# Rotary tables, squares and weight roundings reordered in a kernel's first stretch

## The chip, the cores and the metric

The kernel runs on one core of a Trainium2 chip. The metric is the time of one execution in device microseconds. A core has a matrix engine (TensorE, PE in the profile), a vector engine (VectorE, DVE), an engine for activation functions (ScalarE, ACT), a general engine (GpSimd, POOL) and SyncE (SP), which here issues most of the loads. Each engine works through its own queue in order; ScalarE and GpSimd have DMA queues of their own beside SyncE's.

## The reference

Two layers of a decoder on 512 tokens of width 1024, in float32. What matters here is the beginning of the first one: a norm, one projection whose columns are queries (512), keys (128), values (128) and a gated convolution (3 x 512), and attention in which queries and keys are normed per head and rotated.

```python
def _rope_tables(positions):
    inv_freq = ROPE_THETA ** (-jnp.arange(0, HEAD_DIM, 2, dtype=jnp.float32) / HEAD_DIM)
    ang = positions.astype(jnp.float32)[..., None] * inv_freq
    return jnp.cos(ang)[:, :, None, :], jnp.sin(ang)[:, :, None, :]

h = _rms_norm(x, mix_norm[i])                       # x * rsqrt(mean(x^2) + eps) * gain
q, k, v, cb, cc, cx = _split(h @ w_in, HY_SPLITS)
q = _apply_rope(_rms_norm(q.reshape(b, s, 8, 64), q_norm), cos, sin)
k = _apply_rope(_rms_norm(k.reshape(b, s, 2, 64), k_norm), cos, sin)
# sliding-window attention with sinks, a gated short convolution, an output projection,
# a gated MLP, a per-layer embedding; then a second layer with gated linear attention
```

## The kernel before

Every float32 matrix product is made of three products of rounded operands: each operand is split into a rounded part (hi, an ACTIVATE on ScalarE) and its rest (lo, a subtraction on VectorE), and TensorE adds hi x hi, hi x lo and lo x hi. For weights the split is `cut` (lines 151 and 153), or, in the first stretch, `rounded_w` (line 555), which rounds and returns a function that makes the rest (line 557). The tiles are `raw` (two buffers of 1 MB), `wh` and `wl` (three each).

`mixer0` begins the first layer. Its order is written out by hand inside `tc.manual_schedule` for TensorE, VectorE and ScalarE: the x blocks are transposed (`turn`, line 535, two PSUM banks `turns`), scaled and rounded (`rounded_x`, line 542), their rests made (`rest_x`, line 546), x kept in float32 (`kept`, line 560), while `keys_values` (line 519) and `queries` (line 528) run over the 8 blocks k of the width. Queries 0 to 3 run here; queries 4 to 7 need another 1 MB of weights and run behind, through `mm3` (lines 177 to 179). Ahead of all this `idle` issues matmuls whose result goes nowhere (line 237): four in `setup`, three behind the first transposition. `square` (line 563) sums x squared for the row norm on ScalarE; `end_norm` makes the row factors rtok of them (lines 208 and 209).

What stands outside the hand-written order is placed by a planner that goes by the order of the program text and by its own estimate of when each instruction is ready; it may put such instructions between those of the hand-written order. `tc.issue_after(ins)` keeps instructions behind `ins` on its engine. Before the change the rounding of query weights 4 to 7, two of the four squares, the row norm and the rotary tables stood outside.

`rope_tables` loads the positions through GpSimd's queue (line 416), converts and transposes them (418, 420, 422), makes the angles (426), reduces each to a sine's range (437 to 445), takes sine and cosine on ScalarE (446), and multiplies them by the query and key norms' gains (459 to 464). The keys, scaled by rtok (line 676), are then normed and rotated (651 to 685), transposed by TensorE (667), and the attention and the convolution's projections (line 177 to 179 again, by `conv_in`) follow. The loads that GpSimd issues are held back until the last of x has landed (`late`, line 241).

## Time and profile before

| | |
|---|---|
| median of three runs | 1199.97 us (1198.24 to 1200.52) |
| the profiled execution | 1197.56 us, its span 1195.8 us |
| TensorE busy | 1186.5 us, 99% of the span |
| VectorE, ScalarE, GpSimd busy | 995.1, 693.6, 46.2 us |
| granted TensorE clock | 1.00 |

All times in a timeline are microseconds from the start of the span. The stretch that the change touches ends at about 46 us. A row of a timeline gives start, length, engine, line, operation, what it writes and reads, and in brackets how long the engine stood idle before it and what ended that. A matmul's row shows its length in the pipeline; how fast matmuls follow each other is read from their starts.

### The profile page before, as it was taken

To read this page: it belongs to the slowest core of one execution; us is meant where nothing else is said; L and a number is where in the kernel's file an instruction comes from. 1 tells how busy PE (TensorE), PEld (TensorE's weight loads), DVE (VectorE), ACT (ScalarE), POOL (GpSimd) and SP (SyncE) were. 2 spreads that over 40 slices of the span, in tenths; PEclk is the share of its full clock that TensorE was granted. 3 is DMA by queue.
4 is the path that set the end of the run, shared out by engine and by line. 5 is a ranking of instruction groups with operands and counts; after the bars stand their busy time and mean duration, and the time that the engine had idled before them with its cause. 6 is when DMAs were issued, how large, how long until landed. Compare 5 with 4: busy or idle time off the path is not lost.

```text
span 1195.8 us, 20221 instructions
## 1 busy us (share of the span) xinstructions
PE 1186.5 (99%) x8210; PEld 1077.5 (90%) x8210; DVE 995.1 (83%) x1597; ACT 693.6 (58%) x1140; POOL 46.2 (4%) x65
## 2 busy tenths in 40 slices
PE   9999999999999999999999999999999999999998
PEld 8777789999999989889988988899999999888887
DVE  4986687898999997889879876687989999988595
ACT  6666555556555744666664655555555656655374
POOL 2610000000000000000100000000000000000000
PEclk9999999999999999999999999999999999999999
DMA  7223222332323343422412212223233333323601
GB/s 223 76 80 93 75 89 71 102 111 101 112 83 113 107 141 98 129 74 65 146 59 70 84 59 71 88 74 117 93 112 101 106 107 114 125 89 98 211 1 71
DMA packets 113666, 117.77 MB, mean 98 GB/s; under 512 B 2936, under 2 KB 108594, under 8 KB 113572
## 3 DMA queue, kind: packets, MB, share of 16 engines
q1 hardware_dynamic: 112592, 115.75, 29.9%
q8 instruction: 64, 1.05, 0.4%
q0 software_dynamic: 592, 0.43, 0.3%
q10 hardware_dynamic: 388, 0.30, 0.1%
q14 instruction: 30, 0.25, 0.1%
HBM read 114.37 MB, written 2.10 MB: 97 GB/s over the span
## 4 chain that ended last, share of the span: by engine, by line
PE 86%; DVE 8%; ACT 3%; DMA 1%; issue 1%; POOL 0%; ACTq 0%; DVEq 0%
PE ps L177 7%; PE ps L178 7%; PE ps L179 7%; PE pa L179 6%; PE pa L178 6%; PE pa L177 6%; PE ps L1021 5%; PE ps L1023 5%; PE ps L1022 5%; PE ps L193 5%; PE ps L191 5%; PE ps L200 4%; PE pa L1023 2%; PE pa L1021 2%; PE pa L1022 2%; DVE wl L969 2%
## 5 line engine op out<-in xcount | busy, mean ns | idle before, releaser
L153 DVE TENSOR_TENSOR wl<-raw,wh 128x1024 fp32r<-128x1024 f32 (+2 forms) x132 | 153.8, 1168 | 35.9 <-ACT wh L151 33.7
L151 ACT ACTIVATE wh<-raw 128x1024 fp32r<-128x1024 f32 (+3 forms) x136 | 136.7, 1007 | 64.1 <-PE ps L178 26.9
L966 ACT ACTIVATE wh<-raw 128x1024 fp32r<-128x1024 f32 x90 | 95.8, 1065 | 128.1 <-DVE raw L993 80.2
L1084 DVE SCALAR_TENSOR_TENSOR zt<-z,vfa,zt 128x510 f32<-128x510 f32 (+1 forms) x176 | 131.0, 745 | 0.3
L969 DVE TENSOR_TENSOR wl<-raw,wh 128x1024 fp32r<-128x1024 f32 x90 | 110.1, 1223 | 17.0 <-ACT wh L966 16.0
L179 PE MATMUL pa<-b,wl 128*128 128x256 f32 x352 | 97.3, 276 | 0.1
L179 PE MATMUL pa<-a,wl 128*128 128x256 f32 x352 | 97.3, 276 | 0.0
L177 PE MATMUL pa<-a,wh 128*128 128x256 f32 x352 | 97.2, 276 | 0.0
L178 PE MATMUL pa<-a,wh 128*128 128x256 f32 x352 | 97.2, 276 | 0.0
L177 PE MATMUL pa<-b,wh 128*128 128x256 f32 x352 | 97.2, 276 | 0.0
L178 PE MATMUL pa<-b,wh 128*128 128x256 f32 x352 | 97.2, 276 | 0.0
L1082 ACT ACTIVATE zt<-z,vfb 128x512 f32<-128x512 f32 x88 | 71.5, 813 | 19.1 <-DVE z L1074 9.5
L191 PE MATMUL ps<-b,wh 128*128 128x512 f32 (+1 forms) x192 | 72.9, 383 | 0.0
L193 PE MATMUL ps<-b,wh 128*128 128x512 f32 (+1 forms) x192 | 72.2, 379 | 0.0
L179 PEld LDWEIGHTS pa<-b,wl 128*128 128x128 f32 x352 | 66.1, 188 | 0.3 <-DVE wl L153 0.3
L178 PEld LDWEIGHTS pa<-a,wh 128*128 128x128 f32 x352 | 66.1, 188 | 0.0
L178 PEld LDWEIGHTS pa<-b,wh 128*128 128x128 f32 x352 | 66.1, 188 | 0.0
L177 PEld LDWEIGHTS pa<-a,wh 128*128 128x128 f32 x352 | 66.1, 188 | 0.0
L177 PEld LDWEIGHTS pa<-b,wh 128*128 128x128 f32 x352 | 66.1, 188 | 0.0
L179 PEld LDWEIGHTS pa<-a,wl 128*128 128x128 f32 x352 | 66.1, 188 | 0.0
L1021 PE MATMUL ps<-four,wh 128*128 128x256 f32 x232 | 64.7, 279 | 0.0
L1023 PE MATMUL ps<-four,wl 128*128 128x256 f32 x232 | 64.1, 276 | 0.0
(537 smaller groups left out, 3698.9 us busy)
## 6 DMA issues: line engine op xcount, KB each, us to landing
raw<-in_ffn_w_up_dram SPq DMA_DIRECT2D x42, 1024.0 KB, 5.0
raw<-in_ffn_w_down_dram SPq DMA_DIRECT2D x13, 1024.0 KB, 5.1
raw<-in_gla_w_in_dram SPq DMA_DIRECT2D x8, 1024.0 KB, 5.4
raw<-in_hy_w_in_dram SPq DMA_DIRECT2D x7, 1024.0 KB, 5.0
raw<-in_ffn_w_down_dram SPq DMA_DIRECT2D x8, 768.0 KB, 4.9
raw<-in_ple_w_gate_dram SPq DMA_DIRECT2D x6, 1024.0 KB, 5.4
raw<-in_hy_w_out_dram SPq DMA_DIRECT2D x16, 256.0 KB, 3.9
raw<-in_gla_w_out_dram SPq DMA_DIRECT2D x4, 1024.0 KB, 5.2
```

Source lines behind the costliest of these rows:

```text
L151: nc.scalar.activation(hv, v, AF.Copy)
L153: self.rest_cut = nc.vector.tensor_tensor(lv, v, hv.bitcast(F32), ALU.subtract)
L177: mm(out, lh, rh, start=start, stop=False, **kw)
L178: mm(out, lh, rl, start=False, stop=False, **kw)
L179: mm(out, ll, rh, start=False, stop=stop, **kw)
L191: mm(out, lh, rh, start=first, stop=False, **kw)
L193: end = mm(out, lt, rt, start=False, stop=False, **kw)
L966: nc.scalar.activation(h, src, AF.Copy)
L969: nc.vector.tensor_tensor(l, src, h.bitcast(F32), ALU.subtract)
L1021: mm(out, wh, xh, start=first and j == 0, stop=False, **kw)
L1023: mm(out, wl, xh, start=False, stop=j == ND // 2 - 1, **kw)
L1084: nc.vector.scalar_tensor_tensor(out=y[:, tap:], in0=z[:, : S - tap], scalar=w[:, f : f + 1], in1=y[:, tap:], op0=ALU.mult, op1=ALU.add,)
```

## The change

- `rope_tables` becomes a generator in three parts. The first (positions, their transposition into the bank `turns[1]`, angles, the sine's argument) stands in the hand-written order ahead of `keys_values(4)`, behind the rest of key weights 6 and 7. It gives back the sine as a function, which is called behind the fourth square. The second part (the cosine's argument) follows, with its sine at once. The products with the gains stay behind the row norm.
- `square(2)` is issued ahead of the first part, `square(3)` behind the copies of x blocks 6 and 7, both in the hand-written order. The rest of key weights 6 and 7 moves ahead of the operands' transpositions.
- Query weights 4 to 7 are loaded as before. Their rounding is bound behind `square(3)` for 4 and 5, and behind the last copy of the values for 6 and 7.
- The scaling of the sinks by -1 is bound behind the normed keys.
- The first block of key and value weights is loaded by SyncE, third in its queue behind x block 0, and no longer by ScalarE's queue; the first norm's gains (`vec0`) go through ScalarE's queue and no longer through GpSimd's.
- Two idle matmuls stand behind the first transposition in place of three.

```diff
-        self.kvr = self.raw(ND, 256)
...
-            nc.scalar.dma_start(self.kvr[:, 0, :], a["hy_w_in"][0][:P, 512:768])
...
-        finish = self.columns("vec0", [f(a["mix_norm"])], self.nc.gpsimd)
+        finish = self.columns("vec0", [f(a["mix_norm"])], self.nc.scalar)
...
-    def rope_tables(self, pool):
+    def rope_tables(self, pool, bank):
...
-        ps = self.pa()
-        nc.tensor.transpose(ps[:, :NT], pf, self.ident[:NT, :NT])
+        nc.tensor.transpose(bank[:, :NT], pf, self.ident[:NT, :NT])
         pos = self.cf[:, P : P + NT]
-        nc.vector.tensor_copy(pos, ps[:, :NT])
+        nc.vector.tensor_copy(pos, bank[:, :NT])
+        (the loads of the gains g, moved here from behind the sines)
...
-            nc.scalar.activation(r, r, AF.Sin)
             sc.append(o)
+            yield lambda r=r: nc.scalar.activation(r, r, AF.Sin)
...
-        return C, Sn
+        yield C, Sn
...
-            kvr, wqr = self.kvr, self.raw(4, 512)
+            kvr, wqr = self.raw(ND, 256), self.raw(4, 512)
...
             load_x(0, 1)
+            load_kv(0, 1)
             load_q(0, 1)
...
-                self.idle(3)
+                self.idle(2)
...
                 square(0)
                 square(1)
+                square(2)
+                rest()
+                tables = self.rope_tables(mp, turns[1])
+                sine = next(tables)
                 keys_values(4, 0, 1, 2)
                 turn(6, 7)
                 rounded_x(6)
                 rounded_x(7)
-                rest()
                 rest_x(6)
                 rest_x(7)
                 last = [kept(6, on_act), kept(7, on_dve)]
+                squared = square(3)
+                sine()
+                next(tables)()
                 keys_values(5, 0, 1, 2)
...
-            wq47 = self.weights(w_in[:, 4:8, :512], 4, 512, by="a")
-            wq.update({k: wq47(k - 4, 0, 512) for k in range(4, ND)})
-            with tc.issue_after(last[0].ins):
-                square(2)
-                square(3)
+            wqr = self.raw(4, 512)
+            load(wqr, w_in[:, 4:8, :512])
+            with tc.issue_after(squared.ins):
+                rounded_w(wq, wqr[:, :2], 4, self.weight_tiles())()
             self.end_norm(sums=sums)
-            with tc.issue_after(last[1].ins):
-                C, Sn = self.rope_tables(mp)
+            C, Sn = next(tables)
...
-            nc.vector.tensor_scalar_mul(sink, sink, -1.0)
...
-                nc.scalar.activation(v, pkv[t][:, 128:], AF.Copy, scale=rt)
+                kept_v = nc.scalar.activation(v, pkv[t][:, 128:], AF.Copy, scale=rt)
                 vs.append(v)
+            with tc.issue_after(kept_v.ins):
+                rest = rounded_w(wq, wqr[:, 2:], 6, self.weight_tiles())
+            rest()
...
+            with tc.issue_after(normal.ins):
+                nc.vector.tensor_scalar_mul(sink, sink, -1.0)
```

More of the change, by code (lines that the diff above doesn't have):

```diff
@@ L418, in rope_tables @@
         nc.vector.tensor_copy(pf, pr)
-        ps = self.pa()
-        nc.tensor.transpose(ps[:, :NT], pf, self.ident[:NT, :NT])
+        nc.tensor.transpose(bank[:, :NT], pf, self.ident[:NT, :NT])
         pos = self.cf[:, P : P + NT]
-        nc.vector.tensor_copy(pos, ps[:, :NT])
+        nc.vector.tensor_copy(pos, bank[:, :NT])
+        g = pool.tile([P, 2, HD], F32, name="gqk")
+        for w in range(2):
+            self.late(g[:, w, :1])
+        nc.gpsimd.dma_start(g[:, 0, :], a["hy_q_norm"][0:1, :].partition_broadcast(P))
+        nc.gpsimd.dma_start(g[:, 1, :], a["hy_k_norm"][0:1, :].partition_broadcast(P))
         h = HD // 2
@@ L445, in rope_tables @@
             nc.vector.tensor_scalar(r, r, PI_SAFE, -PI_SAFE, op0=ALU.min, op1=ALU.max)
-            nc.scalar.activation(r, r, AF.Sin)
             sc.append(o)
+            yield lambda r=r: nc.scalar.activation(r, r, AF.Sin)
         sin, cos = sc
-        g = pool.tile([P, 2, HD], F32, name="gqk")
-        for w in range(2):
-            self.late(g[:, w, :1])
-        nc.gpsimd.dma_start(g[:, 0, :], a["hy_q_norm"][0:1, :].partition_broadcast(P))
-        nc.gpsimd.dma_start(g[:, 1, :], a["hy_k_norm"][0:1, :].partition_broadcast(P))
         C = pool.tile([P, NT, 2, HD], F32, name="ropeC")
@@ L562, in square @@
             def square(t):
-                nc.scalar.activation(junk, xin[t // 2][:, t % 2, :], AF.Square, accum_out=sums[:, t : t + 1])
+                return nc.scalar.activation(
+                    junk, xin[t // 2][:, t % 2, :], AF.Square, accum_out=sums[:, t : t + 1]
+                )
             on_act, on_dve = nc.scalar.copy, nc.vector.tensor_copy
@@ L684, in mixer0 @@
             kn = mp.tile([P, 8, HD], F32, tag="qn", name="kn", bufs=2)
-            nc.vector.tensor_tensor(kn, m1, rk.unsqueeze(2).to_broadcast([P, 8, HD]), ALU.mult)
+            normal = nc.vector.tensor_tensor(kn, m1, rk.unsqueeze(2).to_broadcast([P, 8, HD]), ALU.mult)
+            with tc.issue_after(normal.ins):
+                nc.vector.tensor_scalar_mul(sink, sink, -1.0)
             for k in range(4, ND):
```

## The prediction

> **What bounds the kernel now.** I read the page first, then the waits of TensorE, then the timeline of each engine over the first 60 us, where all of the change lies, and last the DMA issues of that stretch. The page and the waits of TensorE (what it waited for: us in total, times, longest):

> ```profile
> span 1195.8 us, 20221 instructions
> PE 1186.5 (99%) x8210; PEld 1077.5 (90%) x8210; DVE 995.1 (83%) x1597; ACT 693.6 (58%) x1140; POOL 46.2 (4%) x65
> PE pa L667 <- DVE kn L685: 2.1, 1, 2.1
> ```

> TensorE is busy for 99% of the span, so time falls only where TensorE stands still or where it works slowly, and rises only where it is made to wait. The list of its waits has the longest first, and that is one stall: the transposition of the normed keys, kn (line 667), waits for VectorE. TensorE's timeline shows its size (start, length, instruction, idle time ahead):

> ```profile
> 43.34 0.39 PE L178 MATMUL ps<-wl,a 128*128 128x512 f32 x1
> 43.57 0.39 PE L179 MATMUL ps<-wh,a 128*128 128x512 f32 x1
> 46.10 0.66 PE L667 MATMUL pa<-cf,kn 128*128 128x128 f32 x4 [2.14 <-DVE kn L685]
> ```

> These matmuls start 0.23 us apart (43.57 - 43.34). Without a wait the transposition would have started at 43.80, so 46.10 - 43.80 = 2.30 us are lost. Why kn is late is read from VectorE:

> ```profile
> 26.12 0.17 DVE L642 TENSOR_SCALAR sink<-sink 128x8 f32<-128x8 f32 x1 [3.55 <-DMA sink<-in_hy_sinks_dram]
> 28.12 1.22 DVE L153 TENSOR_TENSOR wl<-raw,wh 128x1024 fp32r<-128x1024 f32 x1
> 32.89 0.16 DVE L422 COPY cf<-pa 128x4 f32<-128x4 f32 x1 [0.15 <-PE pa L420]
> 33.09 0.68 DVE L426 TENSOR_SCALAR ang<-cf 128x32 f32<-128x32 f32 x4
> 37.15 0.29 DVE L442 SCALAR_TENSOR_TENSOR tabsin<-kksin,tabsin 128x128 f32<-128x128 f32 x1
> 37.48 0.23 DVE L445 TENSOR_SCALAR tabsin<-tabsin 128x128 f32<-128x128 f32 x1
> 43.08 1.11 DVE L655 TENSOR_TENSOR m<-kx,ropeC 128x512 f32<-128x512 f32 x1
> 44.29 1.02 DVE L660 TENSOR_TENSOR m<-m,m 128x512 f32<-128x512 f32 x1
> 45.35 0.69 DVE L685 TENSOR_TENSOR kn<-m,rq 128x512 f32<-128x512 f32 x1
> ```

> VectorE stands still for 3.55 us up to 26.12, at a scaling of the sinks whose load is late. Then it makes the rotary tables between 32.89 and 43.08, mixed with weight rests (the wl of line 153) and with the keys' sums, and only then the keys can be multiplied by ropeC. The tables end late, and kn with them.

> **The tables, part by part.** The position's transposition now stands in TensorE's order between the last of queries(2) and keys_values(4), and VectorE gets the steps up to the sine's argument right behind the rest of key weights 6 and 7, ahead of the operands' rests 6 and 7.

> ```profile
> 17.92 0.52 POOL L416 DMA_DIRECT2D pos_i<-in_positions_dram  x1
> pos_i<-in_positions_dram POOLq DMA_DIRECT2D x1, 2.0 KB, 2.5
> sink<-in_hy_sinks_dram POOLq DMA_DIRECT2D x1, 4.0 KB, 6.5
> 21.88 0.69 DVE L557 TENSOR_TENSOR wl<-raw,wh 128x512 fp32r<-128x512 f32 x1
> 19.52 0.56 POOL L641 DMA_DIRECT2D sink<-in_hy_sinks_dram  x1
> 23.17 0.99 PE L519 MATMUL pa<-wh,a 128*128 128x256 f32 x7
> ```

> The positions land at 17.92 + 2.5 = 20.4. The rest of weights 6 and 7 ends at 22.57, the conversion of so small a tile (no longer than the copy of 0.16) at about 22.8, and TensorE comes to this place at 23.17. So the new wait has 0.4 us to spare on VectorE's side and 2.4 us on the load's. The copy back (0.16), the angles (0.68) and the reduction follow. That reduction takes seven VectorE instructions like the two at 37.15 and 37.48, of 0.23 to 0.29 us and 0.33 apart: 2.0 us, an estimate. The sine's argument is then ready at about 23.4 + 0.2 + 0.7 + 2.0 = 26.3. All of this fills the 3.55 us in which VectorE stood still, and the scaling of the sinks, moved behind kn, no longer blocks anything. The operands' rests 6 and 7, which came behind the sinks at 26.12 + 0.17, now start at 26.3, so nothing behind them gets later. They and the copy of xT 7, three times the 0.69 of line 557, last to about 28.4, and the cosine's eight steps (2.3 us) follow to 30.7.

> ScalarE carries the squares and both sines:

> ```profile
> 25.24 1.27 ACT L542 ACTIVATE a<-pa,vec 128x512 fp32r<-128x512 f32 x2 [1.17 <-PE pa L535]
> 26.76 1.06 ACT L151 ACTIVATE wh<-raw 128x1024 fp32r<-128x1024 f32 x1 [0.25 <-DMA raw<-in_hy_w_in_dram]
> 29.38 1.06 ACT L563 ACTIVATE junk<-xin 128x1024 f32<-128x1024 f32 x1
> 30.34 0.18 ACT L563 ACTIVATION_READ_ACCUMULATOR junk<-xin 128x1 f32 x1
> 30.82 1.05 POOL L209 TENSOR_TENSOR rtok<-rs,mhalf 128x4 f32<-128x4 f32 x1 [8.22 <-DVE rs L208]
> 31.90 0.37 ACT L676 ACTIVATE kx<-pa,rtok 128x128 f32<-128x128 f32 x1 [0.41 <-POOL rtok L209]
> 33.66 0.41 ACT L680 ACTIVATE v<-pa,rtok 128x128 f32<-128x128 f32 x1
> 35.56 1.28 ACT L446 ACT_TABLE_LOAD   x1
> 37.74 0.31 ACT L446 ACTIVATE tabsin<-tabsin 128x128 f32<-128x128 f32 x1 [0.90 <-DVE tabsin L445]
> ```

> A square costs 1.06 plus its sum's read, with the gap about 1.15 us. The third falls into the 1.17 us in which ScalarE waited for TensorE, so it is free. The fourth no longer stands behind the rounding of the query weights (26.76): behind the two operands (25.24 + 1.27 = 26.5) and the copy of xT 6, at most 0.7 like line 557's tile of that size, it starts at 27.2 and ends at 28.4, 2.1 us ahead of today's 30.5. The row norm's power on GpSimd (1.05) then ends between 29.8 and 31.7, by whether VectorE takes its scaling amid or behind the cosine's steps. ScalarE goes on with the table load (1.28), the sine (0.31) and the rounding of query weights 4 and 5 (1.06): 28.4 + 2.65 = 31.05. The eight copies of keys and values (31.90 to 34.07, 2.2 us) end by about 33.9 or earlier, where they do now. What is gained is VectorE: some 5 us of table work leave the stretch behind 31 us and one weight rest of 1.22 enters it. It was busy there without a break, so kn comes some 3.9 us sooner, near 42.1. The keys' products (1.11, 1.02, 0.69) cannot begin before the copies end, so that end is possible. TensorE wants kn at 43.8 less what it gains at the start. The stall goes: **2.30 us**, with about 1.4 us to spare.

> [...]

> What is next late is these weights. Their hi part came at 26.76 and their rest at 28.12; TensorE reads the rest first here:

> ```profile
> 33.12 0.40 PE L178 MATMUL ps<-wl,a 128*128 128x512 f32 x1
> ```

> With 0.25 us gained ahead of it that is 32.87. The rest now ends at 31.05 + 1.22 = 32.3 if VectorE takes it at once: 0.6 us to spare. If the cosine's sine stands ahead of the rounding on ScalarE, 0.3 goes; if four table products (as long as the 0.29 at 37.15) stand ahead of the rest on VectorE, 1.2 goes. I take no stall, and 0 to 1.6 us for the range. Weights 6 and 7 are rounded behind the last v, at about 35.1, their rest by 36.3; TensorE needs it 24 matmuls of 0.23 later, at 38.4. That is covered, and the buffer's next load behind it (issued about 3.5 us later) is first read far later.

> **The start.**

> ```profile
> 3.76 1.21 PE L535 MATMUL pa<-cf,xin 128*128 128x128 f32 x4 [0.37 <-DMA xin<-in_x_dram]
> 4.42 0.42 ACT L555 ACTIVATE wh<-raw 128x256 fp32r<-128x256 f32 x1 [1.20 <-DMA raw<-in_hy_w_in_dram]
> 5.42 0.69 ACT L542 ACTIVATE a<-pa,vec 128x512 fp32r<-128x512 f32 x1 [0.58 <-DVE vec L262]
> 6.13 0.63 PE L237 MATMUL ps<-ones_r 128*128 128x512 f32 x1
> 6.55 1.04 PE L519 MATMUL pa<-wh,a 128*128 128x256 f32 x4
> 7.41 0.66 PE L519 MATMUL pa<-wl,a 128*128 128x256 f32 x4
> 7.91 0.64 PE L519 MATMUL pa<-wh,a 128*128 128x256 f32 x4
> 1.73 0.46 SPq L486 DMA_DIRECT2D raw<-in_hy_w_in_dram  x1
> raw<-in_hy_w_in_dram ACTq DMA_DIRECT2D x1, 128.0 KB, 3.2
> ```

> The first operand is rounded from 5.42 to 6.11, yet the first real matmul starts at 6.55, behind the third idle matmul (6.13). With two, TensorE is free at about 6.0. The key weights take the third place of SyncE's queue, at 1.73, in place of 4.42 - 3.2 = 1.2 on ScalarE's, and land 0.5 later; their rounding ends at about 5.34 in place of 4.84. The gains' column, now loaded through ScalarE's queue, is there by then, so the operand starts at 5.35, ends at 6.04, and the first matmul follows at 6.1. That is 0.45 us sooner. But four matmuls took 7.41 - 6.55 = 0.86 us there and 0.50 us behind 7.41: the early ones run at about half speed, and if the moment of the change is a matter of time, 0.45 us ahead of it is worth only about 0.45 x 0.50 / 0.86 = **0.26 us**. Every later transfer on SyncE moves by one issue (0.46); I cost it at nothing, since no wait of TensorE names a load behind the first x, and if that cover were gone it would cost at most that 0.46.

> [...]

> **The sum.** 2.30 + 0.26 = 2.56 us. The profiled run took 1197.56 us, its span 1195.8 and 1.76 around it; it would become 1195.0. That run lies 2.4 us under the median 1199.97, which is about as much as the runs spread (1198.24 to 1200.52). From the median: 1199.97 - 2.56 = **1197.4**. What a measurement of this kernel can tell from no change is about 0.2%, 2.4 us, so the forecast stands almost on that line.

> **Rivals.**
> (A) As summed: 1197.4, for itself 1196.7 to 1198.2.
> (B) Weights 4 to 7 late: a stall of 0.3 to 1.6 us at line 178, the time 1197.7 to 1199.0. For it: the rest moves from 28.12 to within 0.6 us of its reader. Another way to it is idle time of ScalarE behind the table load: the sine at 37.74 started 0.90 behind the load's end, for its argument, so up to 0.90 of such time may be hidden there, and the rest would end at 33.2, a stall of 0.3. Against it: the rest is written ahead of the table products, so it should come first when it is ready.
> (C) The clock opens late, since one idle matmul is gone from the early activity. It took from 3.76, the first transposition, to 7.41; as long again at half speed loses some 1.8 us: 1199.2. Against it: TensorE would stand for only 0.1 us there.
> (D) The positions late, the slower side. TensorE and VectorE both stop in order at the new place. The sinks' load, of twice the size and issued at 19.52, took 6.5 us. If GpSimd issues the positions as late as that, they land at 26.0, TensorE goes on at 26.3 in place of 22.9, loses 3.4 and ends 0.8 us slower: 1200.8. It decides from a landing at about 25.2. Against it: today's landing at 20.4.
> (E) The change doesn't do what it says: kn still waits, because the planner puts other VectorE work ahead of the keys. Then only the start is left: 1199.7.
> (F) The planner's order shifts in later stretches whose order is not written by hand: anywhere from 3 us better to 4 us worse. Nothing in the profile prices it.

> **How the numbers follow.** A 0.50, B 0.20, C 0.06, D 0.08, E 0.06, F 0.10. The range reaches down to 1196.2 for A with the spread of runs, and up to 1200.2, which takes in B, C and E and leaves out D and the worse part of F. Faster by over 0.2% (under 1197.57): seven tenths of A (its value lies just under the line, and the profiled run's 1197.56 suggests that the three runs lay high), a fifth of B and four tenths of F: 0.35 + 0.04 + 0.04, 0.43. Slower by over 0.2%: half of D, with landings still later than the sinks', and half of F: 0.09. Within: the rest, 0.48.

> **What would show it.** Right: no wait of line 667 on kn, the two L446 sines near 30 us, the third square ending by 25.3, the first keys' matmul near 6.1, still four in 0.86 us there. Wrong: TensorE standing ahead of the positions' transposition near 23 us (D), at the first weight rest near 32.9 (B), slow matmuls after 7.5 (C), or new idle time behind 110 us (F).

## The result, and the profile after

The changed kernel took 1194.92 us (median of 7, 1193.96 to 1197.02) against 1199.97 us (median of 7, 1197.48 to 1201.06): a ratio of 0.9966, with an interval of 0.9953 to 0.9979, so 2.5 to 5.6 us faster. Three later comparisons of the same two kernels gave 0.9973 (0.9962 to 0.9985), 0.9970 (0.9958 to 0.9982) and 0.9971 (0.9959 to 0.9982). Over all of them the means are 1199.26 us for before (93 runs, standard error 0.13) and 1195.87 us for the changed kernel (27 runs, 0.22): **3.4 us faster**. The forecast was 2.56 us and a time of 1197.4, with 1196.2 as the lower end of its range; the gain was larger.

The profiled execution of the changed kernel has a span of 1193.1 us, 2.7 us shorter than the one of before. Its waits of TensorE, and TensorE's timeline at the place of the stall:

```profile
PE ps L235 <- DVE mhalf L224: 1.3, 1, 1.3
PE pa L519 <- ACT a L542: 0.4, 1, 0.4
PE pa L2215 <- ACT oT L2260: 0.3, 1, 0.3
```
```profile
43.84 0.39 PE L178 MATMUL ps<-wl,a 128*128 128x512 f32 x1
44.06 0.39 PE L179 MATMUL ps<-wh,a 128*128 128x512 f32 x1
44.30 0.60 PE L672 MATMUL pa<-cf,kn 128*128 128x128 f32 x4
```

The wait for kn is gone from the list. The transposition (now line 672) follows the last matmul by 0.24 us, the usual distance. On VectorE the sine's argument is made where it stood still, and kn ends at 42.17, 2.1 us ahead of its reader (44.30):

```profile
23.01 0.21 DVE L418 CAST pos_f<-pos_i 4x128 f32<-4x128 int32 x1
24.04 0.16 DVE L421 COPY cf<-pa 128x4 f32<-128x4 f32 x1 [0.82 <-PE pa L419]
26.71 0.23 DVE L449 TENSOR_SCALAR tabsin<-tabsin 128x128 f32<-128x128 f32 x1
30.93 0.29 DVE L460 SCALAR_TENSOR_TENSOR ropeS<-gqk,tabsin 128x128 f32<-128x128 f32 x1 [1.33 <-ACT tabsin L451]
32.15 1.22 DVE L557 TENSOR_TENSOR wl<-raw,wh 128x1024 fp32r<-128x1024 f32 x1
33.62 0.22 DVE L449 TENSOR_SCALAR tabcos<-tabcos 128x128 f32<-128x128 f32 x1
41.48 0.69 DVE L693 TENSOR_TENSOR kn<-m,rq 128x512 f32<-128x512 f32 x1 [0.74 <-POOL rq L209]
```

At the start the first key matmul stands at 6.36 and the clock opens late in this execution (its record first stands at full at 8.68, at 7.46 in the trace of before): the second group of four begins at 7.38, the third at 8.24, so four still take 0.86 us there. In the trace of before this lasted until 7.41.

```profile
5.31 0.42 ACT L555 ACTIVATE wh<-raw 128x256 fp32r<-128x256 f32 x1 [2.09 <-DMA raw<-in_hy_w_in_dram]
6.36 1.22 PE L519 MATMUL pa<-wh,a 128*128 128x256 f32 x4 [0.40 <-ACT a L542]
7.38 1.05 PE L519 MATMUL pa<-wl,a 128*128 128x256 f32 x4
8.24 0.84 PE L519 MATMUL pa<-wh,a 128*128 128x256 f32 x4
```

So this one execution is 0.53 us behind the profiled one of before at 11 us, 1.87 ahead at 66 us: the stall's removal is worth 2.40 there.

### The profile page after: what moved, and what is told of

The parts are those of the page before. It is cut to its first block, busy times and chain, and to the rows that moved or that the text cites. A ratio compares the mean times of both kernels' runs of the same rounds, so it can differ in the third digit from the quotient of the medians.

```text
span 1193.1 us, 20219 instructions
## 1 busy us (share of the span) xinstructions
PE 1186.0 (99%) x8209; PEld 1077.6 (90%) x8209; DVE 992.9 (83%) x1597; ACT 692.3 (58%) x1140; POOL 44.7 (4%) x64
## 3 DMA queue, kind: packets, MB, share of 16 engines
q8 instruction: 64, 1.05, 0.4%
## 4 chain that ended last, share of the span: by engine, by line
PE 88%; DVE 8%; ACT 3%; issue 1%; DMA 0%; POOL 0%; SPq 0%; ACTq 0%
PE ps L177 7%; PE ps L178 7%; PE ps L179 7%; PE pa L179 6%; PE pa L177 6%; PE pa L178 6%; PE ps L1031 5%; PE ps L1033 5%; PE ps L1032 5%; PE ps L191 5%; PE ps L193 5%; PE ps L200 5%; PE pa L1031 2%; PE pa L1033 2%; PE pa L1032 2%; DVE wl L979 1%
## 5 line engine op out<-in xcount | busy, mean ns | idle before, releaser
L153 DVE TENSOR_TENSOR wl<-raw,wh 128x1024 fp32r<-128x1024 f32 (+2 forms) x130 | 151.0, 1164 | 35.3 <-ACT wh L151 29.7
L151 ACT ACTIVATE wh<-raw 128x1024 fp32r<-128x1024 f32 (+3 forms) x134 | 134.3, 1004 | 63.6 <-PE ps L178 27.3
L179 PE MATMUL pa<-b,wl 128*128 128x256 f32 x352 | 97.3, 276 | 0.1
L179 PE MATMUL pa<-a,wl 128*128 128x256 f32 x352 | 97.2, 276 | 0.0
L178 PE MATMUL pa<-b,wh 128*128 128x256 f32 x352 | 97.2, 276 | 0.0
L178 PE MATMUL pa<-a,wh 128*128 128x256 f32 x352 | 97.2, 276 | 0.0
L179 PEld LDWEIGHTS pa<-b,wl 128*128 128x128 f32 x352 | 66.1, 188 | 0.3 <-DVE wl L153 0.3
L178 PEld LDWEIGHTS pa<-b,wh 128*128 128x128 f32 x352 | 66.1, 188 | 0.0
L178 PEld LDWEIGHTS pa<-a,wh 128*128 128x128 f32 x352 | 66.1, 188 | 0.0
L179 PEld LDWEIGHTS pa<-a,wl 128*128 128x128 f32 x352 | 66.1, 188 | 0.0
```

Of the source, the lines that this page charges most:

```text
L151: nc.scalar.activation(hv, v, AF.Copy)
L153: self.rest_cut = nc.vector.tensor_tensor(lv, v, hv.bitcast(F32), ALU.subtract)
L178: mm(out, lh, rl, start=False, stop=False, **kw)
L179: mm(out, ll, rh, start=False, stop=stop, **kw)
```

## The experiments

**Which part: order or start.** order_only is the changed kernel with the start of before, start_only the kernel before with the changed start:

```diff
 start_only, against before
-            nc.scalar.dma_start(self.kvr[:, 0, :], a["hy_w_in"][0][:P, 512:768])
-        finish = self.columns("vec0", [f(a["mix_norm"])], self.nc.gpsimd)
+        finish = self.columns("vec0", [f(a["mix_norm"])], self.nc.scalar)
+            load_kv(0, 1)
-                self.idle(3)
+                self.idle(2)
```

> The new order of tables, squares and roundings alone; the loads of the start and the three idle matmuls as before. Theory 1 (the stall at line 667 goes, 2.3 us, and what was measured beyond it is the start and the spread of runs): about 2.3 us faster in time, the transposition of kn without a wait. Theory 2 (the loads and the idle matmul at the start are worth more than the 0.26 us of the prediction): also 2.3 us. Theory 3 (TensorE's lead is worth more in later stretches): 3.3 us or more, with the lead in the trace growing behind 46 us.

> The kernel before with the start alone: first key weights from SyncE's queue, the norm's gains from ScalarE's, two idle matmuls. Theory 1: between 0.5 us faster and 0.5 us slower, by when TensorE comes to full rate. Theory 2: about 1.8 us faster. Theory 3: as theory 1.

> The kernel before, unchanged, for the spread of runs and a second trace of the start. Theory 1: a ratio of 1 within 0.15%, and the moment at which four 128x256 matmuls go from 0.86 to 0.48 us differs from the first trace's 7.4 us by up to some 1.5 us. Theory 2: that moment is the same in every trace of this kernel.

> The changed kernel, unchanged. Theory 1: 2.0 to 4.0 us faster; full rate again at another moment than in its first trace (8.6 us). Theory 2: 3.5 to 5 us faster. Theory 3: 3.5 to 5 us faster, and the lead over the kernel before again grows by about 0.7 us behind 46 us.

Measured: order_only 0.9970 (0.9959 to 0.9981), start_only 1.0000 (0.9991 to 1.0009), before_again 1.0001 (0.9992 to 1.0011), after_again 0.9973 (0.9962 to 0.9985). The order carries all that can be measured; the start is worth nothing, give or take 1.1 us. But identical kernels differ by 2.9 us in the span of their profiled executions (before 1195.8, before_again 1198.7), and the trace of before_again shows why:

```profile
44.99 0.39 PE L179 MATMUL ps<-wh,a 128*128 128x512 f32 x1
47.38 0.66 PE L667 MATMUL pa<-cf,kn 128*128 128x128 f32 x4 [2.00 <-DVE kn L685]
49.36 0.63 PE L179 MATMUL ps<-a,wl 128*128 128x512 f32 x1
49.79 0.63 PE L177 MATMUL ps<-a,wh 128*128 128x512 f32 x1
51.49 0.41 PE L178 MATMUL ps<-a,wh 128*128 128x512 f32 x1
51.74 0.40 PE L179 MATMUL ps<-a,wl 128*128 128x512 f32 x1
```
```profile
44.70:48.10 3.40, 1.40 (x10) 0.93 (x10) 3.23 (x5) 1.40 (x4) 2.71 (x4) 1.00 0.91 302
48.10:51.50 3.40, 3.40 (x12) 2.72 (x11) 3.40 (x6) 1.96 (x3) 3.29 (x3) 0.50 0.00 1
51.50:54.90 3.40, 3.40 (x16) 2.80 (x15) 3.40 (x5) 1.32 (x2) 3.29 (x4) 1.00 0.00 0
```

The second fence is busy time by stretch (bounds, length, PE, PEld, DVE, ACT, POOL, granted clock, DMA share, GB/s). Behind the stall matmuls of 512 columns start 0.43 us apart (49.36, 49.79) until 51.5, then 0.25 (51.49, 51.74): the granted clock was 0.50 for 3.4 us, after 3.4 us in which TensorE was busy for 1.40. The first profile of before has no such period:

```profile
48.10:51.50 3.40, 3.40 (x17) 2.80 (x16) 3.40 (x5) 0.68 (x2) 3.40 (x4) 1.00 0.00 0
```

start_only shows it too, from 47.1 to 50.5. I aligned the matmuls of each trace with those of before; this is how much later (+) they stand. The opening is where the record of the granted clock first stands at full. At 47 us the half-rate period of before_again and start_only has just begun to tell:

| execution | opening, us | at 11 us | at 47 us | at 66 us |
|---|---|---|---|---|
| before | 7.46 | 0 | 0 | 0 |
| before_again | 10.55 | +1.42 | +1.67 | +2.92 |
| start_only | 9.55 | +0.85 | +1.49 | +2.35 |
| order_only | 10.13 | +1.21 | -1.14 | -1.15 |
| after | 8.68 | +0.53 | -1.86 | -1.87 |
| after_again | 9.34 | +0.60 | -1.81 | -1.82 |
| after_d | 10.46 | +1.24 | -1.12 | -1.13 |

From 11 to 66 us every trace in this table with the new order gains 2.36 to 2.42 us on the first trace, and the two with the half-rate period lose 1.50. The column at 11 us follows the opening, by 0.3 to 0.5 of its delay. In before, each run's mean granted clock tells the period apart: of 86 runs 46 are at 1.000 (mean 1198.2) and 40 below (mean 1200.5; 33 at 0.998 and 7 at 0.999). The two means are further apart than 1.50, and part of that may be the opening: the executions with the period may also be those that open late. A clock of 0.999 alone is no sure sign of it: the trace of after_idle below has 0.999 without such a period, from a clock that falls 2.4 us before the end of its span.

**Is the stall the cause of the half rate?** Twice I filled it with matmuls; once I put a stall into the changed kernel.

```diff
 stall_filled, stall_filled_b, against before
                 pst = bank()
+                for _ in range(fill):      # 9 for kn
+                    nc.tensor.matmul(pst, xg[0][0][:, :P], xg[0][0], start=True, stop=True)
 stall_back, against after
+            for _ in range(8):
+                nc.vector.tensor_copy(m1, m1)
             normal = nc.vector.tensor_tensor(kn, m1, rk...
```

> The kernel before with nine extra matmuls (9 x 0.23 = 2.1 us, result nowhere used) at the place where TensorE waits for kn: the wait stays, the standing still goes. Theory A (the stall of 2.3 us makes the clock fall to half rate for one period of 3.4 us in four of ten executions, which costs 1.7 to 2 us more in those): 0.9 us faster on average, no execution with a granted clock of 0.998 but for the odd one, and a smaller spread. Theory B (the half rate behind the stall is chance and has nothing to do with it): the same time as before, as many executions at 0.998. Theory C (the fill delays kn's transposition): 0 to 0.3 us slower.

> The kernel before with the stall filled once more. If the half rate behind the stall costs 1.7 us in about half of the executions of before: 0.8 us faster than before, and again no execution with 0.998. If it is 0.2 us or less again: the filling matmuls cost about as much as the half rate did, or the half rate costs less than its length says.

> The changed kernel with eight useless copies on VectorE (0.6 us each) ahead of the normed keys' last product, so that TensorE stands still for about 2 to 2.5 us at kn again. If the stall causes the half rate: about half of the executions at a granted clock of 0.998, mean 3.1 us slower than after_d (2.4 for the stall, 1.5 in half of the executions). If the half rate has another cause that the change removed: no more executions at 0.998 than after_d has, 2.3 us slower than it.

stall_back made the stall longer than meant, and its trace has two half-rate periods on end:

```profile
PE pa L672 <- DVE sink L697: 3.6, 1, 3.6
43.20:46.60 3.40, 1.39 (x7) 0.81 (x5) 3.26 (x6) 1.29 (x3) 3.24 (x4) 1.00 0.56 157
46.60:53.40 6.80, 5.25 (x17) 4.51 (x18) 6.61 (x13) 3.54 (x5) 3.52 (x3) 0.50 0.22 77
```

All 11 of its runs had a clock of 0.996 to 0.998; their mean, 1201.2, is 5.3 us above after_d's 1195.9, where 3.1 was expected. Its trace loses 6.3 us to the changed kernel's between 11 and 66 us: 3.7 at the stall (48.15, where the last matmul's start and the usual distance give 44.43) and 2.5 in the half-rate periods. It opened earlier than after_d's trace, by 0.6 us at 11 us, so the two traces are 5.7 apart at 66 us. None of the 22 runs with the stall filled had 0.998, and 4 had 0.999; of 70 runs of before until then 26 had 0.998 and 6 had 0.999. So the stall causes the period, shown from both sides.

What the period is worth in time is less sure. The filled kernel was not faster: 0.9998 (0.9989 to 1.0007) and 0.9997 (0.9989 to 1.0006) where 0.8 to 0.9 us were expected. Its traces agree with before up to 66 us but for the opening (+0.64 at 11 us, +0.68 at 66 us; +0.38 and +0.38) and slip by a further 0.4 to 0.7 at single places later, which traces of other kernels do too. But six of its runs took 1199.7 to 1201.4 at a clock of 1.000, and no run of before at 1.000 took more than 1199.53. So the filled kernel loses time by something other than the half rate, in executions that no trace shows. What that is stays open.

**Which part of the order.** tables_only is order_only with squares and weight roundings put back; squares_only is before with those alone:

```diff
 squares_only, against before
                 square(1)
+                square(2)
...
+                squared = square(3)
...
-            wq47 = self.weights(w_in[:, 4:8, :512], 4, 512, by="a")
+            with tc.issue_after(squared.ins):
+                rounded_w(wq, wqr[:, :2], 4, self.weight_tiles())()
```

> The tables in three parts in the hand-written order and the sinks' scaling moved; squares and weight roundings as before, start as before. By the prediction's steps the tables carry the gain (5 us of VectorE's work moved ahead of 31 us): the wait at line 667 gone or under 0.3 us, 3 us faster like order_only. The rival: the row factors, which come behind the third and fourth square and the rounding of weights 4 and 5, then set kn: a stall of 0.5 to 1.5 us stays, 1 to 2 us faster.

> Squares and weight roundings as changed; the tables and the sinks as before, start as before. By the prediction's steps VectorE stays without a break between 31 and 46 us and kn comes within 0.7 us of where it was: 0 to 1 us faster, with executions at 0.998 left. The rival (the squares set the row factors and so kn): the stall falls by 1.5 us or more, 2 us faster.

tables_only: 0.9975 (0.9965 to 0.9984), no wait for kn, -2.40 us between 11 and 66 us: the tables alone remove the stall. squares_only: 1.0032 (1.0020 to 1.0043), a stall of 5.0 us in its trace and a clock of 0.997 or 0.998 in all six runs. Both rivals fell, and so did the 0 to 1 us faster that was expected of squares_only. For its longer stall VectorE's timeline gives a reason, which no run tests alone:

```profile
33.35 0.16 DVE L422 COPY cf<-pa 128x4 f32<-128x4 f32 x1 [2.31 <-PE pa L420]
34.41 1.22 DVE L557 TENSOR_TENSOR wl<-raw,wh 128x1024 fp32r<-128x1024 f32 x1
```

Without the earlier tables VectorE still stands for the positions' transposition, which TensorE reaches at 33; the weight rest that filled this time before (31.52, line 153) is now tied behind the values and falls among the tables. Behind them three steps for the queries (46.02, 47.22, 47.29) come ahead of kn, which starts at 47.89. The squares and the later rounding are no gain of their own; in the changed kernel they cost nothing that can be measured (order_only 0.9970, tables_only 0.9975).

**The late executions of the changed kernel.** Of its 27 runs two had a clock of 0.998: one of after_again (1197.90) and one of after_c (1198.44), which is the profiled one. Another run of after_c took 1198.10 at 1.000; what delayed it no trace shows.

> The changed kernel once more, to be set against the two kernels with more idle matmuls on the same chip, and for a third trace of it. With the stall (2.30 us) and its half-rate period (1.7 us in about half of the executions) as the whole cause: 3.1 us faster than before on average. If 4.1 us, as first measured, is right: something is still missing.

```profile
PE pa L419 <- DVE pos_f L418: 2.3, 1, 2.3
24.52 0.21 DVE L418 CAST pos_f<-pos_i 4x128 f32<-4x128 int32 x1 [2.83 <-DMA pos_i<-in_positions_dram]
18.59 0.37 SPq L640 DMA_DIRECT2D raw<-in_hy_w_in_dram  x1
19.82 0.53 POOL L416 DMA_DIRECT2D pos_i<-in_positions_dram  x1
21.70:25.10 3.40, 1.06 (x6) 0.58 (x5) 0.26 (x2) 2.61 (x6) 2.37 (x6) 1.00 1.11 223
25.10:28.50 3.40, 3.40 (x17) 3.40 (x18) 2.58 (x12) 0.00 (x0) 0.43 (x1) 0.50 0.90 290
```

Here the clock had opened at 4.63. TensorE was early, GpSimd was late (1.22 us for the copy ahead of its loads, from 17.38, against 0.17 in the first trace), the 1 MB load of query weights went out at 18.59, ahead of the positions (19.82), and these took until 24.4. In the first trace of the changed kernel the order was the other way round (18.62 and 19.99) and they had landed at 20.9. The stall of 2.3 us and a half-rate period behind it followed. So the wait that the change adds at the positions is real, in one of the four traces. pos_early issues that load at once:

```diff
-        self.late(pr[:, :1])
         nc.gpsimd.dma_start(pr, a["positions"][0].rearrange("(t p) -> t p", p=P))
```

> The changed kernel with the positions' load issued at once by GpSimd instead of behind the last of x. If the positions' late landing makes the changed kernel's late executions: none at 0.998, the largest time under 1197, mean 0.2 to 0.4 us below after_d. Rival (the late executions come from elsewhere): the same spread as after_d. If the early 2 KB load disturbs the first loads of x: up to 0.3 us slower.

> The changed kernel as it is, to be set against the three others on the same chip: 3.0 to 3.6 us faster than before, one or two executions in ten at 0.998 or above 1197.5.

pos_early 0.9965 (0.9952 to 0.9977), at most 1196.07, mean 1195.38; after_d 0.9971 (0.9959 to 0.9982), at most 1196.72, mean 1195.93, and none of its six runs was late either. Five and six runs don't show that the late executions are gone, and the two means (standard errors 0.26 and 0.22) are not clearly apart.

**The clock at the start.** after_idle and after_idle_b are the changed kernel with more matmuls that only keep TensorE busy at the start; after_idle_kv has five and three, with the first key weights on ScalarE's queue ahead of the gains; pos_early_idle is pos_early with six and three.

```diff
 after_idle, after_idle_b, against after (in setup, and ahead of the first keys)
-        self.idle(4)
+        self.idle(6)
...
-                self.idle(2)
+                self.idle(3)
```

> The changed kernel with six idle matmuls in place of four ahead of the first x and three in place of two behind its transposition: TensorE is busy nearly without a break from 1.3 us. Theory A (the clock opens at the end of a period in which TensorE was busy enough, and the periods run freely): the first full-rate matmul between 5 and 8.2 us in place of 7.4 to 10.6, up to 1.2 us faster than the changed kernel, some 4.3 us faster than before. Rival (a matter of the time since the first matmul or of the real work alone, or the extra idle matmuls stand in the way): no faster than the changed kernel, 3.3 us faster than before, or 0.4 us worse than that.

> Six and three idle matmuls again, a second measurement and a second opening moment. If early activity opens the clock sooner: opening between 4.5 and 8 us, 0.5 to 1.2 us faster than after_c. If the first one's 7.29 us was luck: the same time as after_c, opening between 7.4 and 10.7.

> The changed kernel with five and three idle matmuls, the first key weights again through ScalarE's queue (second) and the gains behind them (third). First key matmul near 6.1 us in place of 6.2 to 6.7. If the idle matmuls open the clock sooner and this start is not in the way: within 0.3 us of after_idle_b or better. Rival: with one idle matmul less the activity doesn't suffice, and it ends with after_c.

> The positions early and six and three idle matmuls. If both hold: 4 to 4.8 us faster than before, mean 1 us below after_d, opening of the clock before 8 us. If the idle matmuls' gain was luck: like pos_early.

after_idle opened at 7.29, after_idle_b at 4.18, pos_early_idle at 7.50, and they took 0.9965 (0.9953 to 0.9978), 0.9960 (0.9948 to 0.9972) and 0.9960 (0.9946 to 0.9973). The ten runs of the first two have a mean of 1194.9, 1.0 us under the changed kernel's 1195.87. after_idle_kv opened at 10.56 and took 0.9976 (0.9967 to 0.9984), a mean of 1196.45 us: 0.6 above the changed kernel's 1195.87 over all runs, level with after_c's 1196.42 beside it. That is on the side of its rival; whether the queue or the one idle matmul less did it, no run separates. pos_early_idle's mean, 1194.98, is 0.95 us under after_d's and 0.4 under pos_early's, and the latter is within the noise. Six and three idle matmuls on the changed kernel have the lowest mean here, 4.4 us under before's.

## Why the prediction was wrong

- **The stall, 2.30 us: its size was right.** It is gone, and the traces give 2.36 to 2.42 us between 11 and 66 us. tables_only shows that the tables carry it. kn ended at 42.17 where 42.1 was worked out, but by another path, so that this end fits to 0.1 us is luck. The steps came later than said: the sine's argument at 26.9 (said 26.3), the fourth square at 29.3 (28.4), the cosine's argument at 33.8 (30.7), the latter because VectorE took table products ahead of it and stood 1.33 us for the sine. The cosine then stood amid the copies of keys and values, which ended at 35.2 (said 33.9). And VectorE was not busy without a break: it stood still for 0.38, 1.08 and 0.74 us between 33.8 and 41.5. The last of these was for rq, the keys' factors, which GpSimd makes from the keys' sums; the prediction has no such wait. Against these 2.2 us stand 1.2 for a weight rest, which stood ahead of kn before the change (41.02) and came behind it (42.17), and 0.8 for the keys' first two products, which were shorter than the 1.11 and 1.02 taken.

```profile
33.87 0.31 ACT L451 ACTIVATE tabcos<-tabcos 128x128 f32<-128x128 f32 x1 [1.00 <-DVE tabcos L449]
34.83 0.38 ACT L685 ACTIVATE v<-pa,rtok 128x128 f32<-128x128 f32 x1
39.27 0.68 DVE L660 TENSOR_TENSOR m<-kx,ropeC 128x512 f32<-128x512 f32 x1
40.05 0.69 DVE L665 TENSOR_TENSOR m<-m,m 128x512 f32<-128x512 f32 x1
39.43 2.02 POOL L209 TENSOR_TENSOR rq<-rs,mhalf 128x8 f32<-128x8 f32 x1 [2.97 <-DVE rs L208]
42.17 1.22 DVE L153 TENSOR_TENSOR wl<-raw,wh 128x1024 fp32r<-128x1024 f32 x1
```

- **The start, 0.26 us: its first step came, its worth is not shown.** The first key matmul stood at 5.92 to 6.36 in the four traces of the changed kernel, 6.1 on average as said, against 6.55 and 6.63 before. But the opening moment moves between 4.6 and 10.6 us from one execution to the next, 1 us of it being worth 0.3 to 0.5 us, and start_only can't tell the start from nothing. What sets that moment is not shown: with seven idle matmuls in all it was 7.46 (before), 10.55 (before_again) and 10.13 (order_only), with six 8.68, 9.34, 4.63 and 10.46 (the changed kernel's traces), and no run separates the time from the early matmuls. So the 0.26, which takes it for a matter of time, and rival C, which takes it for a matter of the idle matmuls, were the author's estimates.
- **The step that failed: the sum had no term behind the stall.** It took TensorE to go on at full rate, as it did in the one execution shown. In 40 of 86 runs of before the mean clock says that it went on at half rate, which cost 1.50 us in the two traces that show it: 0.7 us on average. 2.40 + 0.70 = 3.1, against 3.4 measured (standard error 0.25); what is left is within the noise. That the half rate follows from the stall is shown; that its end is worth 0.7 us in the mean is worked out from traces, and the filled kernel, which lost the period but gained nothing, leaves it open. Only a clock that opens late was among the rivals (C), at the start and as a loss.
- **The time, 2.5 us too high.** Three things add up. The median of three that it started from, 1199.97, lies 0.7 above the mean of 93 runs, and two of the three lay where the half-rate runs of before are. The gain was 0.8 larger than 2.56. And the first comparison's median, 1194.92, lies 1.0 under the mean of 27 runs, for which nothing but the spread of runs is known. Against that mean, 1195.87, the range's end of 1196.2 was still missed by 0.3. Between executions without the period the forecast's 2.56 about holds: 1198.2 for the 46 runs of before at 1.000, 1195.7 for the 25 of the changed kernel above 0.998.
- **Rival B** didn't come: the rest of weights 4 and 5 ended at 33.37, a us later than said, and TensorE did not wait. **Rival D** came in one trace of four, with its stall of 2.3 us, and there the order of the two loads was turned round (18.59 and 19.82); its price there was the stall and a half-rate period more. They landed at 24.4, short of the 25.2 that the prediction names, and that execution (1198.44) still lay under the mean of before.
- **Rival B's other way**, idle time of ScalarE behind the table load, didn't come either. In the changed kernel the load starts 0.02 us behind the sum's read (29.27) and ends at 30.57, and the sine starts at 30.58:

```profile
29.08 0.19 ACT L563 ACTIVATION_READ_ACCUMULATOR junk<-xin 128x1 f32 x1
29.29 1.28 ACT L451 ACT_TABLE_LOAD   x1
30.58 0.31 ACT L451 ACTIVATE tabsin<-tabsin 128x128 f32<-128x128 f32 x1
```

## What to carry to other kernels

Price a stall of TensorE like this one (2.0 to 2.3 us) with what the clock takes behind it (here 1.5 us in the two traces that show it, and by the mean clock up to 40 of 86 runs have it), and look at more than one execution: a profile can be one of those in which it did not happen. Where VectorE stands still early and is the bound later, work that depends on nothing late (tables) is worth moving by hand. When such work needs a small load earlier, look at which large loads can get ahead of it; issuing it at once, as in pos_early, cost nothing here (a mean of 1195.38 against 1195.93), though it isn't shown to help.

## What the runs showed of the hardware

How busy TensorE was in a period, by the profile, then went with what the next one had. Behind 0.00 (squares_only), 1.07 (after_c), 1.40 (start_only), 1.41 (before_again) and 1.42 us (stall_back) of 3.41 the clock fell. Behind 2.37 and 2.31 us, the two parts of the first trace's stall, it stayed. In stall_back the first half-rate period held 1.84 us, and a second followed. Where the line lies between is not measured.

Beyond that, executions slip by 0.3 to 0.8 us at single places behind 390 us, in kernels with and without the change; what these are was not looked into.
